# Grouped-query attention on one core: ten output staging buffers in place of four, and the copies of K into its padded form on the GpSimd DMA queue

## The chip, the cores and the metric

The kernel runs on one core of one Trainium2 chip. The metric is device time in microseconds (us) of one execution. The engines named below are PE (TensorE), ACT (ScalarE), DVE (VectorE), POOL (GpSimd) and SP (SyncE). SP does no arithmetic here: it only issues DMAs, in the order of its instruction stream, each when the semaphores it waits for have come.

## The reference

```python
batch, n_q_heads, n_kv_heads, seq, head_dim = (8, 8, 2, 1024, 64)
scale = 1.0 / np.sqrt(head_dim)
for g in range(n_kv_heads):                 # 4 query heads share one K and one V
    scores = scale * np.matmul(q_group, k_group.transpose(0, 1, 3, 2))
    scores_max = np.max(scores, axis=-1, keepdims=True)
    attn = np.exp(scores - scores_max)
    attn = attn / (np.sum(attn, axis=-1, keepdims=True) + 1e-08)
    output[:, q_start:q_end, :, :] = np.matmul(attn, v_group)
```

Inputs and output are float32; the kernel works in bf16 and takes no maximum off, since the scores are small.

## The kernel before, in words

A head's Q is 1024 x 64. It is cast to bf16 by a DMA from DRAM to DRAM on POOL's queue (`cast`, L248) and read back as 512 rows of 128 numbers, each row two neighbouring queries. Two transposing DMAs on SP (L260, 256 rows each) put it into SBUF as `qT`, 128 x 512: the upper 64 partitions hold the even queries, the lower 64 the odd ones. One job is one head and one `side` (even or odd queries), so there are 8 x 8 x 2 = 128 jobs of 512 queries.

K of a batch and group is cast and transposed in the same way into `kT`. A score matmul contracts over all 128 partitions and must see one side only, so K is kept with zeros in the other half of the partitions: `kset`, for each side. `place_k` (L267) copies `kT` there with four small DMAs (64 partitions x 512 bf16), one for each side and parity. There are 16 pairs of batch and group; the first is made on chip by `first_loads`, the other 15 come by `place_k`: 60 DMAs. V is read from its bf16 copy by two DMAs (`place_v`, L282). `kset` and `vset` have two sets, by the batch's parity.

A job has eight cells, one for each 128 keys. A cell's scores are one matmul (L351) into PSUM. 824 of the 1024 cells get their exponential on ACT (L362, two cells at a time, 412 instructions), 200 on DVE, where bits are put together (L371) and corrected for four cells at a time in four steps (L386, L392, L402, L406). Each cell's exponentials then go through four matmuls with V and a column of ones (L414), which gather output and row sums in one of two PSUM banks. When a job's eight cells are done, `normalise` takes the reciprocal of the sums (L427), multiplies into a staging tile `ost` (L429, 128 x 256 float32), and SP stores that tile (L435, 128 KB). The next multiply into the same staging buffer waits until that store has landed; a PSUM bank comes free for a later job when L429 has read it.

All is recorded in an order that `make_plan` writes out ahead of time. Casts, transposes, `place_k` and `place_v` are put in at fixed distances from the planned first use of a head, `th`:

```python
at(th - 28.0, cast, ("q", b, h), q[b, h])
at(th - 17.0 + n, transpose_q, b, h, n)
at(th - 38.0, cast, ("k", b, g), k[b, g])
at(th - 33.0, cast, ("v", b, g), v[b, g])
at(th - 27.0 + n, transpose_k, b, g, n)
at(th - 20.0, place_k, b, g, side, parity)
at(th - 15.0, place_v, b, g)
```

The order on each engine is the order of this plan. A cast also waits for the score matmul recorded last before it (`last_score`), so POOL's queue keeps pace with PE. SP has no such pace: it takes its DMAs one after another.

Of the kernel before, what the change touches and what calls it, by code (L numbers as in the profile page):

```python
# [162 lines left out]
def kernel(  # L163
# [7 lines left out]
    nc = tc.nc  # L171
# [38 lines left out]
    pa_pool = ctx.enter_context(tc.tile_pool(name="papool", bufs=26))  # L210
    pd_pool = ctx.enter_context(tc.tile_pool(name="pdpool", bufs=6))
    tmp_pool = ctx.enter_context(tc.tile_pool(name="tmppool", bufs=2))
    ostage_pool = ctx.enter_context(tc.tile_pool(name="ostage", bufs=4))
    recip_pool = ctx.enter_context(tc.tile_pool(name="recip", bufs=4))

    def psum_pools(name, n):
        return [
# [47 lines left out]
        transpose(("k", b, g), kT[(b, g)], n)  # L265

    def place_k(b, g, side, parity):  # L267
        nc.sync.dma_start(
            out=ksets[b % 2][
                side * D : (side + 1) * D, g, side, parity * HALF : (parity + 1) * HALF  # L270
            ],
            in_=kT[(b, g)][parity * D : (parity + 1) * D, :],
        )
# [179 lines left out]
    for b in range(B):  # L453
        for h in range(H):
            if b == 0 and h == 0:
                continue
            th = first_use[(b * H + h) * 2]
            if (b, h) != (0, 1):
                at(th - 28.0, cast, ("q", b, h), q[b, h])
            for n in range(HALF // PIECE):  # L460
                at(th - 17.0 + n, transpose_q, b, h, n)
            if h % HPG == 0:
                g = h // HPG
                at(th - 38.0, cast, ("k", b, g), k[b, g])
                at(th - 33.0, cast, ("v", b, g), v[b, g])
                for n in range(HALF // PIECE):
                    at(th - 27.0 + n, transpose_k, b, g, n)
                for side in range(2):
                    for parity in range(2):
                        at(th - 20.0, place_k, b, g, side, parity)  # L470
                at(th - 15.0, place_v, b, g)
# [34 lines left out]
```

## Time and profile before

| | |
|---|---|
| Time, median of 2 runs | 442.2 us (439.77 to 444.63) |
| The profiled execution: its time | 446.41 us |
| The profiled execution: its span | 444.6 us |
| Mean granted TensorE clock | 0.967 of full |

The span runs from the first to the last instruction; 1.8 us of the profiled execution's time lie around it. Idle time of an engine is put down to what ended it. A DMA issue counts as no engine's busy time, but the trace gives its start and how long the issuing queue was held by it, and when the data had landed.

### The profile page before, as it was taken

What the parts mean: (1) busy time and instruction counts of PE and PEld (TensorE: products, weight loads), DVE (VectorE), ACT (ScalarE), POOL (GpSimd) and SP (SyncE); (2) the same over time, 40 slices, a digit from 0 to 9 for tenths busy, and PEclk for the clock granted to TensorE, in tenths of its full rate; (3) what the DMA queues carried; (4) which work ended last, traced back from release to release, by engine and by line L of the source; (5) the groups of instructions that cost most, each with busy time, mean ns of one, the idle gap of its engine ahead of it and who ended that gap; (6) DMA issues with size and microseconds to landing.
All of it is one profiled execution on the core that took longest, in us unless ns stands there. A gap on an engine that the chain in (4) does not pass through costs nothing.

```text
span 444.6 us, 12769 instructions
## 1 busy us (share of the span) xinstructions
PE 383.3 (86%) x5132; PEld 235.5 (53%) x5132; DVE 376.2 (85%) x664; ACT 386.1 (87%) x415; POOL 55.8 (13%) x105
## 2 busy tenths in 40 slices
PE   4888799699998989898788969998969998797995
PEld 2445465355655546555455535565636665454654
DVE  5897698599997979699698859989959997897994
ACT  4898699599998979899899968998949999797992
POOL 5401001001111110111111110110101111100000
PEclk9999899799999989999999997999969999999998
DMA  3754666647665675656747555574655747645314
GB/s 94 125 98 94 115 110 111 116 91 126 100 125 104 111 119 97 120 93 114 119 84 126 109 107 102 97 130 97 121 107 98 119 83 135 111 89 111 82 29 84
DMA packets 137771, 46.73 MB, mean 105 GB/s; under 512 B 130848, under 2 KB 136224, under 8 KB 136224
## 3 DMA queue, kind: packets, MB, share of 16 engines
q1 hardware_dynamic: 134208, 33.46, 36.6%
q0 software_dynamic: 2976, 12.20, 20.9%
q8 instruction: 40, 0.66, 0.7%
q10 hardware_dynamic: 528, 0.26, 0.2%
q14 instruction: 19, 0.16, 0.1%
HBM read 27.13 MB, written 28.97 MB: 126 GB/s over the span
## 4 chain that ended last, share of the span: by engine, by line
DVE 32%; PE 26%; DMA 15%; ACT 13%; SPq 8%; issue 4%; POOL 1%; DVEq 0%; ACTq 0%
PE aps L351 14%; ACT pa L362 13%; DMA out_dram<-ost 11%; PE ops L414 9%; DVE y L402 7%; DVE pd L406 6%; SPq L260 6%; DVE pd L371 6%; DVE ost L429 5%; DVE y L392 4%; PE dps L351 3%; DVE z L386 2%; DMA qT<-scr_q 2%; DVE rec L427 1%; SPq L282 1%
## 5 line engine op out<-in xcount | busy, mean ns | idle before, releaser
L362 ACT ACTIVATE pa<-aps 128x1024 bf16<-128x1024 f32 x412 | 383.6, 1045 | 45.6 <-PE aps L351 44.0
L351 PE MATMUL aps<-qT,kset 128*128 128x512 bf16 x824 | 252.2, 389 | 13.5 <-ACT pa L362 9.7
L414 PEld LDWEIGHTS <-pa 128*128 128x128 bf16 x3296 | 137.7, 98 | 91.8 <-DVE ost L429 20.8
L414 PE MATMUL ops<-vset,pa 128*128 128x65 bf16 x3296 | 149.1, 195 | 29.5 <-DVE ost L429 29.4
L371 DVE TENSOR_SCALAR pd<-dps 128x512 uint16<-128x512 f32 x200 | 129.6, 680 | 2.4 <-PE dps L351 2.1
L351 PEld LDWEIGHTS <-kset 128*128 128x128 bf16 x1024 | 85.2, 99 | 68.1 <-issue 34.7
L429 DVE TENSOR_TENSOR ost<-ops,rec 128x256 f32<-128x256 f32 x128 | 54.3, 424 | 49.7 <-DMA out_dram<-ost 46.0
L248 POOL DMA_DIRECT2D scr_q<-in_q_dram x63 | 35.2, 558 | 300.7 <-PE aps L351 265.1
L351 PE MATMUL dps<-qT,kset 128*128 128x512 bf16 x200 | 66.6, 389 | 0.3
L406 DVE TENSOR_TENSOR pd<-pd,y 128x2048 uint16<-128x2048 uint16 x50 | 61.2, 1225 | 1.7
L402 DVE TENSOR_TENSOR y<-z,y 128x2048 f16<-128x2048 uint16 x50 | 61.2, 1225 | 1.7
L414 PEld LDWEIGHTS <-pd 128*128 128x128 bf16 x800 | 38.0, 97 | 39.4 <-DVE pd L406 20.1
L414 PE MATMUL ops<-vset,pd 128*128 128x65 bf16 x800 | 45.4, 194 | 8.5 <-DVE pd L406 7.4
L392 DVE TENSOR_SCALAR y<-z 128x2048 f16<-128x2048 uint16 x50 | 34.3, 687 | 0.6
L386 DVE TENSOR_SCALAR z<-pd 128x2048 uint16<-128x2048 uint16 x50 | 34.2, 684 | 0.0
L427 DVE RECIPROCAL rec<-ops 128x4 f32<-128x4 f32 x128 | 22.3, 174 | 5.5 <-PE ops L414 5.4
L248 POOL DMA_DIRECT2D scr_k<-in_k_dram x15 | 7.8, 519 | 22.7 <-PE aps L351 17.0
L248 POOL DMA_DIRECT2D scr_v<-in_v_dram x15 | 7.7, 515 | 15.8 <-PE aps L351 15.2
L321 PE MATMUL dps<-ident,hk 128*128 128x128 bf16 x8 | 1.0, 310 | 4.9 <-DVE hk L313 4.9
L309 POOL MEMSET kset<- 64x2048 bf16 x2 | 3.6, 1798 | 0.1
L321 PEld LDWEIGHTS <-hk 128*128 128x128 bf16 x8 | 0.8, 140 | 4.9 <-DVE hk L313 4.9
L236 DVE MEMSET kset<- 64x1024 uint32 x2 | 1.8, 912 | 1.3 <-PEq L490 1.0
(19 smaller groups left out, 7.9 us busy)
## 6 DMA issues: line engine op xcount, KB each, us to landing
out_dram<-ost SPq DMA_DIRECT2D x128, 128.0 KB, 2.7
scr_q<-in_q_dram POOLq DMA_DIRECT2D x63, 128.0 KB, 3.2
kset<-kT SPq DMA_DIRECT2D x60, 64.0 KB, 2.9
qT<-scr_q SPq DMA_TRANSPOSE x126, 3.5
scr_k<-in_k_dram POOLq DMA_DIRECT2D x15, 128.0 KB, 3.2
scr_v<-in_v_dram POOLq DMA_DIRECT2D x15, 128.0 KB, 3.7
vset<-scr_v SPq DMA_DIRECT2D x30, 64.0 KB, 3.2
kT<-scr_k SPq DMA_TRANSPOSE x30, 3.3
```

Source lines behind the costliest of these rows:

```text
L248: dma = nc.gpsimd.dma_start(out=scr.rearrange("(p f) -> p f", f=1024), in_=src.rearrange("(p s) d -> p (s d)", s=1024 // D),)
L260: nc.sync.dma_start_transpose(out=dst[:, rows], in_=src[rows, :])
L351: last_score[0] = nc.tensor.matmul(dst, lhsT=ksets[b % 2][:, h // HPG, side, c * 128 : (c + 1) * 128], rhs=qT[(b, h)], start=True, stop=Tr ...
L362: nc.scalar.activation(out=pt[:, 0:m], in_=psum.pop(("A", n))[:, 0:m], func=AF.Exp, scale=scale)
L371: nc.vector.tensor_scalar(out=groups[g][:, slot], in0=psum.pop(cell), scalar1=bits_scale, scalar2=bits_bias, op0=ALU.mult, op1=ALU.add,)
L386: nc.vector.tensor_scalar(out=z, in0=pd, scalar1=0x7F, scalar2=None, op0=ALU.bitwise_and)
L392: nc.vector.tensor_scalar(out=y, in0=temps[g][0], scalar1=CURVE_A / 128.0, scalar2=CURVE_B, op0=ALU.mult, op1=ALU.add,)
L402: nc.vector.tensor_tensor(out=y, in0=z, in1=y, op=ALU.mult)
L406: nc.vector.tensor_tensor(out=pd, in0=pd, in1=y, op=ALU.add)
L414: nc.tensor.matmul(ops_of[s][:, qs, :], lhsT=p_of[cell][:, qs * 128 : (qs + 1) * 128], rhs=vsets[b % 2][:, h // HPG, c, :], start=opens an ...
L427: nc.vector.reciprocal(out=rec, in_=o[:, :, D])
L429: nc.vector.tensor_tensor(out=ost, in0=o[:, :, 0:D], in1=rec.unsqueeze(2).to_broadcast([128, NQS, D]), op=ALU.mult,)
```

## The change

The pools of the staging tile `ost` and of the reciprocals get ten buffers in place of four. The four DMAs of `place_k` are issued by POOL in place of SP; their data, their shapes and what they wait for stay.

```diff
@@ -210,8 +210,8 @@
-    ostage_pool = ctx.enter_context(tc.tile_pool(name="ostage", bufs=4))
-    recip_pool = ctx.enter_context(tc.tile_pool(name="recip", bufs=4))
+    ostage_pool = ctx.enter_context(tc.tile_pool(name="ostage", bufs=10))
+    recip_pool = ctx.enter_context(tc.tile_pool(name="recip", bufs=10))
@@ -265,7 +265,7 @@
     def place_k(b, g, side, parity):
-        nc.sync.dma_start(
+        nc.gpsimd.dma_start(
             out=ksets[b % 2][
                 side * D : (side + 1) * D, g, side, parity * HALF : (parity + 1) * HALF
             ],
```

On SP, at the second of the 15 bursts of `place_k` (the DMAs into `kset_114`, the set of the odd batches), before (-) and now (+):

```order
 L260 DMA_TRANSPOSE kT<-scr_k 128x256 x2
 L260 DMA_TRANSPOSE qT<-scr_q 128x256 x2
-L435 DMA out_dram<-ost 128x4x64
-L268 DMA kset_114<-kT 64x512 x4
-L435 DMA out_dram<-ost 128x4x64 x2
+L435 DMA out_dram<-ost 128x4x64 x3
 L260 DMA_TRANSPOSE qT<-scr_q 128x256 x2
 L282 DMA vset_112<-scr_v 128x4x64 x2
```

The burst leaves SP, and the stores and transposes behind it follow one another.

On POOL, at the first burst (into `kset_109`, the set of the even batches; `scr_q`, `scr_k` and `scr_v` are the bf16 copies in DRAM that the casts write):

```order
 L248 DMA scr_q<-in_q_dram 16x4096
 L248 DMA scr_v<-in_v_dram 16x4096
-L248 DMA scr_q<-in_q_dram 16x4096 x3
+L248 DMA scr_q<-in_q_dram 16x4096 x2
+L268 DMA kset_109<-kT 64x512 x4
+L248 DMA scr_q<-in_q_dram 16x4096
 L248 DMA scr_k<-in_k_dram 16x4096
 L248 DMA scr_q<-in_q_dram 16x4096
 L248 DMA scr_v<-in_v_dram 16x4096
```

The burst now stands in POOL's order behind two casts and ahead of the third cast of Q and of the next cast of K; it waits there until `kT` has landed. All 15 bursts stand so.

On DVE, at the sixth and seventh stores into `ost`, with what each waits for:

```order
 L427 RECIPROCAL rec<-ops_524 128x4 [waits PE_49]
-L429 TENSOR_TENSOR ost<-ops_524,rec 128x256 [waits DMAHW4_49,DVE_49]
+L429 TENSOR_TENSOR ost<-ops_524,rec 128x256 [waits DVE_49]
 L371 TENSOR_SCALAR pd<-dps_614 128x512
 L386 TENSOR_SCALAR z<-pd 128x2048
 L427 RECIPROCAL rec<-ops_623 128x4 [waits PE_49]
-L429 TENSOR_TENSOR ost<-ops_623,rec 128x256 [waits DMAHW0_49,DVE_49]
+L429 TENSOR_TENSOR ost<-ops_623,rec 128x256 [waits DVE_49]
```

The waits for the landing of an earlier store (DMAHW) are gone here; from the eleventh job on they are there again, for the store ten jobs back. The order of PE, ACT and DVE is the same in both kernels.

## Rows read from the trace of the kernel before

**Rows 1.** The page: busy us of each engine, share, instructions.

```profile
PE 383.3 (86%) x5132; PEld 235.5 (53%) x5132; DVE 376.2 (85%) x664; ACT 386.1 (87%) x415; POOL 55.8 (13%) x105
```

**Rows 2.** Waits: who waited <- for whom: us, times, longest.

```profile
DVE ost L429 <- DMA out_dram<-ost: 46.0, 21, 5.1
ACT pa L362 <- PE aps L351: 44.0, 37, 4.5
...
PE ops L414 <- DVE pd L406: 7.4, 13, 0.9
...
PE aps L351 <- DMA qT<-scr_q: 1.7, 2, 1.3
```

**Rows 3.** Timeline, DVE, PE, ACT (start, us, line, count [idle before <-releaser]).

```profile
71.45 0.42 DVE L429 TENSOR_TENSOR ost<-ops,rec 128x256 f32<-128x256 f32 x1
...
85.30 0.42 DVE L429 TENSOR_TENSOR ost<-ops,rec 128x256 f32<-128x256 f32 x1 [4.73 <-DMA out_dram<-ost]
...
85.78 0.60 PE L414 MATMUL ops<-vset,pa 128*128 128x65 bf16 x8 [3.81 <-DVE ost L429]
...
87.33 1.02 ACT L362 ACTIVATE pa<-aps 128x1024 bf16<-128x1024 f32 x1 [4.48 <-PE aps L351]
```

**Rows 4.** Timeline of SP's queue between those two L429.

```profile
72.42 3.33 SPq L268 DMA_DIRECT2D kset<-kT  x4
75.85 0.54 SPq L435 DMA_DIRECT2D out_dram<-ost  x1
76.49 4.10 SPq L260 DMA_TRANSPOSE qT<-scr_q  x2
80.68 1.08 SPq L282 DMA_DIRECT2D vset<-scr_v  x2
81.85 1.01 SPq L435 DMA_DIRECT2D out_dram<-ost  x2
```

**Rows 5.** SP's queue: first and last row between 30 and 410, and the last transposes.

```profile
30.93 1.12 SPq L260 DMA_TRANSPOSE qT<-scr_q  x1
...
408.10 2.42 SPq L260 DMA_TRANSPOSE qT<-scr_q  x2
...
412.04 3.27 SPq L260 DMA_TRANSPOSE qT<-scr_q  x2
```

**Rows 6.** SP's queue: the first and the last burst of `place_k`.

```profile
22.42 3.85 SPq L268 DMA_DIRECT2D kset<-kT  x4
...
394.00 3.21 SPq L268 DMA_DIRECT2D kset<-kT  x4
```

**Rows 7.** Lines L260 and L248: ns of one issue, min/median/max.

```profile
L260 SPq DMA_TRANSPOSE qT<-scr_q x126: 1105/1228/3302, 6.1 to 414.1; - x126
...
L248 POOL DMA_DIRECT2D scr_q<-in_q_dram x63: 486/486/996, 1.3 to 398.9; - x63
```

**Rows 8.** Timeline: POOL's longest cast issue, and DVE beside it.

```profile
111.62 1.00 POOL L248 DMA_DIRECT2D scr_q<-in_q_dram  x1 [4.10 <-PE aps L351]
...
111.84 0.68 DVE L392 TENSOR_SCALAR y<-z 128x2048 f16<-128x2048 uint16 x1
```

**Rows 9.** POOL's casts behind the first and third burst; SP's issues that go with them.

```profile
16.79 0.49 POOL L248 DMA_DIRECT2D scr_k<-in_k_dram  x1 [1.74 <-PE aps L351]
...
69.65 0.49 POOL L248 DMA_DIRECT2D scr_q<-in_q_dram  x1 [5.25 <-PE dps L351]
...
15.71 3.13 SPq L260 DMA_TRANSPOSE kT<-scr_k  x2
...
39.30 2.44 SPq L260 DMA_TRANSPOSE kT<-scr_k  x2
...
87.39 1.13 SPq L260 DMA_TRANSPOSE qT<-scr_q  x1
```

**Rows 10.** DMA issues: KB each, median us from issue to landing.

```profile
scr_k<-in_k_dram POOLq DMA_DIRECT2D x15, 128.0 KB, 3.2
...
kT<-scr_k SPq DMA_TRANSPOSE x30, 3.3
```

## The prediction

> **What bounds the kernel now.** Busy time does not say: PE, DVE and ACT stand within 10 us of one another, each some 60 us under the span of 444.6 [rows 1]. The waits say more. DVE sat 46.0 us in 21 waits of L429 for a store to land, and ACT 44.0 us for scores [rows 2]. One stall read in order of time shows that these are one chain: the multiply at 85.30 waited 4.73 us, PE's output matmuls at 85.78 then had waited 3.81 us for it, and ACT at 87.33 had waited 4.48 us [rows 3].
>
> Why was the store late? The multiply at 85.30 needs the buffer of the job four before, filled at 71.45 [rows 3]. Its store was issued only at 81.85, ten microseconds after the data stood there. What SP did in between is [rows 4]: a burst of `place_k` (3.33 us), a store, two transposes (4.10), two loads of V (1.08), each starting some 0.1 us after the one before ended. SP never idled; the store stood in a line. And so through the run: the 202 rows of SP's timeline that start between 30 and 410, of which the first and the last are shown [rows 5], add up to 364.0 us in a stretch of 380, and the remaining 16 us are the tenth of a microsecond ahead of each. **SP's issue queue is full, and it is the bound.** DVE's wait for staging buffers is how the rest of the chip is held down to SP's pace. PE was held up for Q by only 1.7 us in two waits [rows 2], so SP was never so late that its transposes mattered much; the stores felt it first.
>
> **The change, part by part.**
>
> *Ten buffers.* L429 waits for a store ten jobs back in place of four. The 128 jobs share a span of 444.6 us, 3.5 us each, so a store may land some 30 us after its data stand before DVE feels it; the shown one took 13 us, from 71.87 to just before 85.30 [rows 3]. This takes the wait off DVE, but makes SP no shorter: by itself it would only hand the lateness to the transposes, for which PE would wait.
>
> *`place_k` off SP.* The 15 bursts hold SP 3.85 us (first) to 3.21 us (last) [rows 6]; all 15 rows add up to 50.1 us, and with 0.1 us ahead of each it is 51.6. That is time of the bounding queue, so it counts in full, unless the moved DMAs slow what stays.
>
> From these follow three ends for the span.
> - SP: its last transposes ended at 412.04 + 3.27 = 415.3 [rows 5], 29.3 us ahead of the end of the span. Without the bursts they can end at 415.3 - 51.6 = 363.7, so SP alone would allow 363.7 + 29.3 = 393.0.
> - DVE: 444.6 - 46.0 = 398.6 if all its waits for stores go [rows 2].
> - ACT: 444.6 - 44.0 = 400.6 if all its waits for scores go [rows 2].
>
> The largest stands: 400.6. All of ACT's gap cannot go, though. PE also waits 7.4 us for DVE's L406 [rows 2], which has nothing to do with stores, and with the other cover gone that reaches ACT. Between none and all of it I take half, 3.7 us: a span of 404.3, with 400.6 and 408.0 as this term's ends. For the granted clock, 0.967 of full over the span, I count nothing: what it costs lies within ACT's waits.
>
> *What POOL pays.* A cast holds POOL 0.49 us at the median, 1.00 at most [rows 7]. The trace has no `place_k` on POOL; I take 0.5 to 1.0 us each from those rows, 2 to 4 us a burst. POOL is busy 13% of the span [rows 1], so the 60 issues are hidden by its idle time. What is not plainly hidden is the wait. In POOL's new order a burst stands ahead of casts and waits for `kT` to land. At the first burst SP's `kT` transposes were issued from 15.71 to 18.84 and land 3.3 us after issue [rows 9, 10], so POOL stands until about 21 to 22 and is through with the burst at 24 to 26; the cast of K that ran at 16.79 [rows 9] moves 7 to 10 us later. Who waits for them? SP reads that K at 39.30; the cast lands 3.2 us after issue [rows 9, 10], so it may be some 19 us late. At the third burst the cast of Q at 69.65 is read at 87.39 [rows 9], 14 us after landing if that takes 3.2 us as K's does; SP issued the burst itself at 72.42 [rows 4], so on POOL it would be through by 74 to 76 at the latest, 5 to 7 us of delay. SP's lateness is the cover here. If SP catches up, the cover shrinks, but then `kT` lands earlier too and POOL waits less. I take zero; without cover a burst would cost up to 4 us, 60 in all.
>
> *A rule against this part.* POOL's longest cast issue, 1.00 us from 111.62, ended at 112.62, just behind DVE's L392 (111.84 to 112.52) [rows 8]. The Trainium skill, SBUF — State Buffer, Who interferes with whom, says that DVE and GpSimd take an exclusive lock on a shared port pair and the later one stands until the other is through; its advice is to issue DMAs from SP or ACT rather than from GpSimd. The trace agrees about the half microsecond. By the rule each moved DMA could cost up to one L392 of 0.68 us more, 41 us in all, but on POOL, which has it to spare; the sum stays.
>
> *The time.* 404.3 of span and 1.8 around it make 406.1 for an execution like the profiled one, which took 446.4 where the runs' median is 442.2. I take 3 of these 4.2 us off: **403 us**.
>
> **The rivals.**
>
> *SP gets back only half.* Transposes take 1.23 us at the median but up to 3.30 [rows 7]. The two at 76.49 took 4.10 [rows 4], 1.6 more than two medians, in a stretch with casts on POOL's queue. If each of the 15 bursts, now itself on POOL's queue, stretches SP's issues beside it by that much, SP loses 25 of the 51.6 us, and its end is 393.0 + 25 = 418. For it: the moved bytes still pass through the same DMA engines. Against it: they did so before. Its times are 410 to 428.
>
> *SP's issue time is not its own.* If SP is held by the DMA engines rather than by the number of its instructions, the freed 51.6 us are filled by longer issues of the others, and PE waits for Q in place of DVE for buffers: 442. Against it: the short stores in the same line (0.54 at 75.85 [rows 4]) show that most issues are not held. The Trainium skill, DMA: Bandwidth & Descriptors, Issuing engines are not separate DMA queues, says that issuing from several engines saves only sequencer time, usually small beside the DMA. That is this rival: the move would gain nothing, 442. The trace disagrees on "small": 364 us of issuing in 380.
>
> *POOL becomes the line that is waited in.* This one ends slower. A burst on POOL holds the casts behind it; SP then waits for a cast at its next transposes, with stores and the next `kT` behind them, and the next burst waits for that `kT`. It decides where a burst delays POOL by more than the 14 us that a cast waits to be read in mid-run, that is at about 3.5 us for each of the four DMAs, where casts show 0.49. At 5 us each, 20 a burst, 6 us are uncovered 15 times: 90 us on a span of 400.6, about 490. At 4.5 us each it is 60 us, about 460. Against it: the longest issue on POOL was 1.00 us.
>
> **How the numbers follow.** The forecast (three nearly equal bounds, 396 to 410) gets 0.66, half relief (410 to 428) 0.24, no relief 0.06, POOL as the line 0.04. The low end, 395, is DVE's 398.6 with 1.8 around it and the 4.2 us by which the profiled run lay above the median taken off, 396.2, less one for the spread of the runs. The high end goes into half relief as far as 422, since its first twelve microseconds hold most of its chance. Two per cent, about what a measurement of this kernel can tell from no change, is 433.4 to 451.0; forecast and half relief lie below, so 0.90 faster, 0.06 the same, 0.04 slower.
>
> **What would show it.** In the new profile L429 should wait for stores almost nowhere; SP's queue should show idle stretches, or still be full but with PE rarely waiting for `qT`; the bursts on POOL should take 2 to 4 us; ACT's busy share should pass 93%, and the clock's mean 0.98 of full. I am wrong if SP stays full and PE's waits for `qT` grow to tens of microseconds (rivals one and two), or if SP's transposes wait for casts (rival three).

## The result and the profile after

The changed kernel takes 397.55 us (median of 2 runs, 397.35 to 397.74) where the kernel before took 442.2: a ratio of 0.899, 95% interval 0.878 to 0.920. With more runs on one chip it was 397.5 against 444.54, ratio 0.894 (0.890 to 0.898). The profiled execution has a span of 395.6 us against 444.6, and a mean granted clock of 0.999 against 0.967.

The busy times, in the page's first part, answer [rows 1]:

```profile
span 395.6 us, 12683 instructions
...
PE 365.7 (92%) x5043; PEld 233.0 (59%) x5132; DVE 375.8 (95%) x664; ACT 381.5 (96%) x415; POOL 86.6 (22%) x165
```

PE, DVE and ACT do the same work in 49 us less. (89 of PE's 824 score matmuls have no record in this trace, x5043 for x5132, so its busy time reads somewhat low.) The waits (who waited <- for whom: us, times, longest) answer [rows 2]:

```profile
POOL kset L268 <- DMA kT<-scr_k: 68.7, 14, 8.6
...
PE aps L351 <- ACT pa L362: 13.6, 44, 0.6
...
ACT pa L362 <- PE aps L351: 1.3, 2, 1.1
...
PE aps L351 <- DMA qT<-scr_q: 0.3, 1, 0.3
```

DVE's 46.0 us for stores have no row any more, ACT's 44.0 us for scores have become 1.3, and PE now waits a little for ACT. The one long wait, POOL's for `kT`, is new. The stretch that held the shown stall [rows 3] now reads, in ACT's timeline and in the busy times of the stretch from 80 to 100 us (us, then PE, PEld, DVE, ACT and POOL busy with their counts, clock, DMA share, GB/s):

```profile
74.28 126.21 ACT L362 ACTIVATE pa<-aps 128x1024 bf16<-128x1024 f32 x137
...
80.00:100.00 20.00, 18.88 (x284) 12.40 (x288) 19.52 (x36) 20.00 (x23) 5.08 (x10) 1.00 0.78 127
```

137 exponentials run for 126 us without a gap. Before, the same stretch had PE 15.70, DVE 14.67 and ACT 14.61 us busy, at a granted clock of 0.83 of full: it fell from 2.4 to 1.2 GHz at 83.94, while PE stood in the wait of [rows 3], and came back at 90.77. In all, 31.6 us of the span before passed at 1.2 GHz, and of the changed kernel's only the last 2.5. SP's queue, beside [rows 4], has lost its bursts:

```profile
81.50 3.28 SPq L260 DMA_TRANSPOSE kT<-scr_k  x2
84.88 2.47 SPq L260 DMA_TRANSPOSE qT<-scr_q  x2
87.45 1.71 SPq L435 DMA_DIRECT2D out_dram<-ost  x3
89.27 3.53 SPq L260 DMA_TRANSPOSE qT<-scr_q  x2
92.90 1.55 SPq L282 DMA_DIRECT2D vset<-scr_v  x2
94.55 1.01 SPq L435 DMA_DIRECT2D out_dram<-ost  x2
```

It is still without a gap: its 174 rows that start between 30 and 360 us add up to 313.1 us, and with the tenth of a microsecond ahead of each they fill the stretch. A store is issued 4.8 us after its data stand (median over 128; before 6.55). But its last transposes now end at 367.3 in place of 415.3, and PE waits only 0.3 us for what they bring. On POOL, beside [rows 9], a burst takes 2.1 to 2.3 us (one of the 15 takes 5.6, since POOL stood idle 2.9 us within it), and the casts behind the first one came at 24.40 and 24.89 in place of 14.07 and 16.79:

```profile
22.12 2.29 POOL L268 DMA_DIRECT2D kset<-kT  x4 [8.64 <-DMA kT<-scr_k]
24.40 0.52 POOL L248 DMA_DIRECT2D scr_q<-in_q_dram  x1
24.89 0.53 POOL L248 DMA_DIRECT2D scr_k<-in_k_dram  x1
...
63.12 2.07 POOL L268 DMA_DIRECT2D kset<-kT  x4 [5.67 <-DMA kT<-scr_k]
65.18 0.52 POOL L248 DMA_DIRECT2D scr_q<-in_q_dram  x1
```

### The profile page after: what moved, and what is told of

It is laid out like the page before. It is cut to its first block, busy times and chain, and to the rows that moved or that the text cites. A ratio compares the mean times of both kernels' runs of the same rounds, so it can differ in the third digit from the quotient of the medians.

```text
span 395.6 us, 12683 instructions
## 1 busy us (share of the span) xinstructions
PE 365.7 (92%) x5043; PEld 233.0 (59%) x5132; DVE 375.8 (95%) x664; ACT 381.5 (96%) x415; POOL 86.6 (22%) x165
## 4 chain that ended last, share of the span: by engine, by line
ACT 67%; DVE 11%; PE 10%; issue 6%; DMA 3%; POOL 1%; SPq 0%
ACT pa L362 67%; PE ops L414 5%; PE aps L351 5%; DVE pd L371 3%; DVE y L402 2%; DVE pd L406 2%; DVE ost L429 1%; DMA vf<-in_v_dram 1%; PE dps L351 1%; DVE y L392 1%; DMA qT<-scr_q 1%; POOL kset L309 1%; DVE z L386 1%; DVE rec L427 1%; DMA scr_q<-in_q_dram 1%
## 5 line engine op out<-in xcount | busy, mean ns | idle before, releaser
L362 ACT ACTIVATE pa<-aps 128x1024 bf16<-128x1024 f32 x412 | 379.0, 1064 | 2.1 <-PE aps L351 1.3
L351 PE MATMUL aps<-qT,kset 128*128 128x512 bf16 x735 | 226.2, 379 | 15.5 <-ACT pa L362 13.6
L414 PEld LDWEIGHTS <-pa 128*128 128x128 bf16 x3296 | 134.5, 97 | 57.6 <-DVE ost L429 0.8
L414 PE MATMUL ops<-vset,pa 128*128 128x65 bf16 x3296 | 143.9, 193 | 3.4
L248 POOL DMA_DIRECT2D scr_q<-in_q_dram x63 | 34.0, 540 | 173.4 <-PE aps L351 150.6
L351 PE MATMUL dps<-qT,kset 128*128 128x512 bf16 x200 | 64.5, 380 | 1.0
L406 DVE TENSOR_TENSOR pd<-pd,y 128x2048 uint16<-128x2048 uint16 x50 | 61.2, 1225 | 1.7
L429 DVE TENSOR_TENSOR ost<-ops,rec 128x256 f32<-128x256 f32 x128 | 54.3, 425 | 4.4
L268 POOL DMA_DIRECT2D kset<-kT x60 | 32.2, 545 | 76.7 <-DMA kT<-scr_k 68.7
L392 DVE TENSOR_SCALAR y<-z 128x2048 f16<-128x2048 uint16 x50 | 34.3, 687 | 0.6
L386 DVE TENSOR_SCALAR z<-pd 128x2048 uint16<-128x2048 uint16 x50 | 34.2, 684 | 0.0
L248 POOL DMA_DIRECT2D scr_v<-in_v_dram x15 | 7.6, 505 | 8.2 <-PE aps L351 7.1
L248 POOL DMA_DIRECT2D scr_k<-in_k_dram x15 | 8.1, 542 | 4.7 <-PE aps L351 4.3
```

Source lines behind the costliest of these rows:

```text
L248: dma = nc.gpsimd.dma_start(out=scr.rearrange("(p f) -> p f", f=1024), in_=src.rearrange("(p s) d -> p (s d)", s=1024 // D),)
L268: nc.gpsimd.dma_start(out=ksets[b % 2][side * D : (side + 1) * D, g, side, parity * HALF : (parity + 1) * HALF], in_=kT[(b, g)][parity * D ...
L351: last_score[0] = nc.tensor.matmul(dst, lhsT=ksets[b % 2][:, h // HPG, side, c * 128 : (c + 1) * 128], rhs=qT[(b, h)], start=True, stop=Tr ...
L362: nc.scalar.activation(out=pt[:, 0:m], in_=psum.pop(("A", n))[:, 0:m], func=AF.Exp, scale=scale)
L386: nc.vector.tensor_scalar(out=z, in0=pd, scalar1=0x7F, scalar2=None, op0=ALU.bitwise_and)
L392: nc.vector.tensor_scalar(out=y, in0=temps[g][0], scalar1=CURVE_A / 128.0, scalar2=CURVE_B, op0=ALU.mult, op1=ALU.add,)
```

## The experiments

Each ran beside the kernel before on the same chip (444.1 to 445.1 us there).

| run | time, us | ratio to before (95%) | span | SP's DMA issues, sum |
|---|---|---|---|---|
| before (profile) | | | 444.6 | 381.3 |
| bufs_only | 437.0 | 0.983 (0.976 to 0.990) | 437.8 | 381.3 |
| half_place | 406.3 | 0.914 (0.908 to 0.920) | 402.4 | 344.5 |
| place_only | 401.4 | 0.904 (0.898 to 0.910) | 398.8 | 339.7 |
| changed kernel (after_again) | 397.5 | 0.894 (0.890 to 0.898) | 395.6 | 335.2 |
| place_six | 397.6 | 0.898 (0.890 to 0.905) | 396.0 | 337.5 |
| place_x4 | 398.4 | 0.900 (0.893 to 0.906) | 396.8 | 310.4 |
| v_too | 397.9 | 0.895 (0.890 to 0.900) | 396.0 | 301.0 |

The last column adds up how long each DMA issue held SP's queue. The span and the sum of the changed kernel are those of its first profile.

**Which half does it.** Ten buffers alone, then the move alone:

```diff
# bufs_only: the kernel before, with
+    ostage_pool = ctx.enter_context(tc.tile_pool(name="ostage", bufs=10))
+    recip_pool = ctx.enter_context(tc.tile_pool(name="recip", bufs=10))
```

> Ten buffers alone, place_k stays on SP. Theory 1 (SP's issue time is the bound of the kernel before, 364 us of issuing in 380): nothing leaves SP's queue, so the span stays at 436 to 446 us; DVE's 46.0 us of waits for stores shrink, and PE's waits for qT (1.7 us before) grow to some 40 us in their place. Theory 2 (four buffers were the bound, SP merely busy): DVE's waits go and nothing takes their place, 397 to 405 us.

```diff
# place_only: the changed kernel, with
+    ostage_pool = ctx.enter_context(tc.tile_pool(name="ostage", bufs=4))
+    recip_pool = ctx.enter_context(tc.tile_pool(name="recip", bufs=4))
```

> place_k on POOL alone, with four buffers. Theory 1 (SP's issue time): SP is relieved by 51.6 us, a store stands in line some 5 us as in the changed kernel, where four jobs at 3 us each leave 12 us for line and landing; a few waits for stores remain, under 10 us in all: 397 to 407 us. Theory 2 (the buffers): four buffers still hold DVE, 435 to 444 us.

Both came out as the theory of SP's issue time has it. The waits of bufs_only:

```profile
ACT pa L362 <- PE aps L351: 38.1, 30, 3.3
PE aps L351 <- DMA qT<-scr_q: 30.4, 18, 2.8
DVE rec L427 <- PE ops L414: 25.7, 29, 3.1
```

DVE no longer waits for stores, but PE's matmuls wait 30.4 us for Q, DVE for PE, and ACT nearly as long as before. SP's last transposes end at 414.9 (before 415.3): the wait has only changed its place. What the buffers did bring, 7 us of span, lies almost all behind that point, 22.9 us to the end in place of 29.3. The clock is no rival here: a run of bufs_only with a mean granted clock of 0.992 still took 436.6 us. In place_only DVE waits 4.4 us for stores in 6 waits, and the time is 4 us above that with ten buffers:

```profile
DVE ost L429 <- DMA out_dram<-ost: 4.4, 6, 1.5
```

**How much of SP's time counts.** Half of the burst goes back:

```diff
# half_place: the changed kernel, with
-        nc.gpsimd.dma_start(
+        (nc.sync if side == 0 else nc.gpsimd).dma_start(
```

> Ten buffers; two of each burst's four DMAs (side 0) go back to SP, two stay on POOL. Theory 1 (SP's issue time is paid in full): 30 DMAs at 0.86 us (51.6 us for 60) bring back 26 us. SP's last transposes in the changed kernel end near 366 us, then near 392, and with the 29.3 us behind them the span is 415 to 424 us; PE waits for qT some 20 us. Rival (SP has room left and only a whole burst hurts): 396 to 402 us.

406.3 us lies between the two. The 30 returned DMAs held SP 18.1 us (0.60 each, not 0.86), and the others shrank by nearly 9 us: the 30 transposes of K from 47.8 to 39.9 us, the stores from 84.1 to 81.2. So SP's last transposes end at 377.2, 10 us later than in the changed kernel and not 25. PE's matmuls wait 5.8 us for Q, in 4 waits. With ten buffers the first 30 DMAs cost 9 us and the other 30 cost 31 (bufs_only): the price of SP's time is not straight. Where SP is the bound it is nearly so: from half_place to bufs_only the sum of issues grows by 36.8 us and the span by 35.4.

**Six buffers.** 

```diff
# place_six: the changed kernel, with
+    ostage_pool = ctx.enter_context(tc.tile_pool(name="ostage", bufs=6))
+    recip_pool = ctx.enter_context(tc.tile_pool(name="recip", bufs=6))
```

> place_k on POOL with six staging buffers in place of ten. If a store needs the line on SP (median 4.8 us, at most 8.6 in the changed kernel) and 3.2 us to land, it is through within 12 us, and six jobs at 3 us give 18: no wait for a store, 396 to 399 us, the same as with ten. If ten buffers are needed because lateness comes in long stretches: waits of DVE for stores of over 5 us and 401 us or more.

397.6 us, and no row of DVE waiting for a store: with the burst gone from SP six are as good as ten.

**POOL's cover.** Each `place_k` in four parts:

```diff
# place_x4: the changed kernel, with
+        for p in range(0, D, 16):
+            nc.gpsimd.dma_start(
+                out=ksets[b % 2][
+                    side * D + p : side * D + p + 16, g, side, parity * HALF : (parity + 1) * HALF
+                ],
+                in_=kT[(b, g)][parity * D + p : parity * D + p + 16, :],
+            )
```

> The changed kernel with each place_k cut into four DMAs of 16 partitions: 240 issues on POOL in place of 60, same bytes. By the cover theory a burst takes POOL about 16 x 0.545 = 8.7 us in place of 2.2, casts behind it come up to 6.5 us later, and they are read 10 us (median) but at least 3.0 us after landing: a few stalls at most, 396 to 404 us. By the rival of the prediction (POOL becomes the line that is waited in) the cover is used up at every burst: over 410 us, with PE's waits for qT growing by more than 10 us.

398.4 us, under a microsecond more, with POOL 45% busy; PE waits 0.3 us for Q, in its weight loads. SP did wait: for 9 of the 63 heads it started the transposes of Q within 0.1 us of the landing of their cast, where the changed kernel has 2. So casts came too late for SP several times, and still not for PE.

**What bounds the changed kernel.** First SP, by moving V's loads too:

```diff
# v_too: the changed kernel, with
-            nc.sync.dma_start(
+            nc.gpsimd.dma_start(
                 out=vsets[b % 2][:, g, two * NHC : (two + 1) * NHC, 0:D],
```

> The changed kernel with the 30 loads of V on POOL's queue as well. Theory A (ACT, busy 381.5 of 395.6 us and idle 2.1 us ahead of its exponentials, is now the bound): SP is freed of another 20 us and its stores stand in line shorter than the 4.8 us median, with idle stretches on its queue, and the time stays at 396 to 399 us. Theory B (SP, whose rows fill 333 of 335 us between 30 and 365, is still the bound): 375 to 390 us.

397.9 us, no change, though SP's issues fall by 34 us in sum (V's loads had 19.0 of it; the stores fall by 16.7 as well) and its queue idles at last, as here for 3.1 us between two rows of its timeline:

```profile
229.12 1.17 SPq L260 DMA_TRANSPOSE qT<-scr_q  x1
233.43 0.37 SPq L435 DMA_DIRECT2D out_dram<-ost  x1
```

SP is not the bound of the changed kernel. Then, on the kernel of v_too, less work for ACT, for DVE, for both, and for PE as well:

```diff
# act_light: 52 cells' exponentials left out
-        m = len(cells)
+        m = 1 if n % 8 == 0 else len(cells)
...
-            p_of[cell] = pt[:, col, :]
+            p_of[cell] = pt[:, min(col, m - 1), :]
# dve_light: the step of L386 left out
-            z = tmp_pool.tile([128, GROUP, QBS], U16, name="z")[:, 0:m]
-            temps[g] = [z]
-            nc.vector.tensor_scalar(
-                out=z, in0=pd, scalar1=0x7F, scalar2=None, op0=ALU.bitwise_and
-            )
+            temps[g] = [pd]
...
-                scalar1=CURVE_A / 128.0,
+                scalar1=1e-4,
# three_light: act_light and dve_light, and the scores of those 52 cells
+            if col == 1 and n % 8 == 0:
+                return
```

> The kernel with V's loads on POOL too (397.85 us, SP out of the way), and every eighth ACT exponential takes one of its two cells; the other cell's output matmuls use the same exponentials. This leaves out 52 cells' exponentials, some 23 us of ACT. If ACT is the bound: 376 to 390 us, down to where DVE's 376 us of busy time stop it. If DVE holds it alone: 396 to 399 us.

> The same base, and DVE leaves out the 50 masking steps (L386, 0.68 us each, 34 us); the next step reads the unmasked bits. If ACT alone is the bound: 395 to 399 us, with DVE's busy share down from 95% to 87%. If DVE is a bound beside it, the time falls too: 380 to 394 us.

> The changed kernel as it is, beside these two on the same chip: 397 to 398 us.

> Both omissions together, 52 cells' exponentials on ACT and the 50 masking steps on DVE. Alone they gave 1.4 us and nothing, while ACT's busy time fell by 16.7 us and DVE's by 26. If ACT and DVE are two bounds side by side, each standing in when the other is lightened: 379 to 387 us, ACT's 364.8 us and the 14 us in which it idles at both ends. If a third bound (PE, at 92%) holds both: 393 to 398 us.

> As with both omissions, and the score matmul of the 52 cells whose exponentials are left out is left out too: 52 x 0.215 us, some 11 us of PE. The theory that ACT and DVE are the two bounds side by side has fallen (395.5 where 379 to 387 was expected). If PE, which shows matmuls back to back from 200 to 212 us there, is the third bound: 383 to 389 us. If it is neither of the three but the order in which they wait for one another: 392 to 396 us.

| run | time, us | busy PE / DVE / ACT, us |
|---|---|---|
| v_too | 397.9 | 365.4 / 376.2 / 381.5 |
| act_light | 396.1 | 363.5 / 375.0 / 364.8 |
| dve_light | 397.9 | 364.0 / 350.0 / 381.4 |
| both_light | 395.5 | 363.3 / 349.7 / 364.5 |
| three_light | 394.2 | 363.8 / 349.2 / 365.0 |

The changed kernel beside the first two took 397.5 us. These misses say most. Against v_too, ACT's work cut by 17 us gave 1.7; DVE's by 26 us nothing; both together 2.4; with some 11 us of PE's scores cut too, 3.6. (PE's busy time does not show that cut: the traces of the other four lack 89 records of score matmuls, that of three_light lacks none.) No engine's length is the bound by itself, and the theory of two bounds side by side fell. The chain of work that ended last, followed back from the last instruction, changes hands (shares of the span by engine): in the changed kernel it is

```profile
ACT 67%; DVE 11%; PE 10%; issue 6%; DMA 3%; POOL 1%; SPq 0%
```

in act_light

```profile
DVE 49%; PE 36%; ACT 8%; issue 4%; DMA 2%; ACTq 0%
```

and in three_light

```profile
ACT 59%; PE 33%; issue 6%; DMA 1%; DVE 0%; ACTq 0%
```

The waits of three_light show the other side:

```profile
PE aps L353 <- ACT pa L364: 15.1, 57, 0.6
ACT pa L364 <- PE aps L353: 14.7, 55, 0.7
```

PE waits for ACT 57 times and ACT for PE 55 times, a quarter of a microsecond each. With scores passing through two PSUM buffers in an order written ahead, each engine sets the pace in its own stretches. That it is this order is argued from these rows; no run changed the order or the number of PSUM buffers (all eight banks are taken), so it stays open.

## Why the prediction was right

**The bound.** That SP's issue queue holds the kernel before, and DVE's wait for buffers is only how it shows, is what bufs_only and place_only test, and both came out inside what this theory gave. Ten buffers alone moved DVE's wait to PE; the move without the buffers gave nine tenths of the gain. That SP's rows fill the run does not show it by itself: they fill it in the changed kernel too, where SP is not the bound. (The 364.0 us for 202 rows count three rows twice: it is 360.6 us for 199, with 18.9 us between them; the reading stands.) Whether an issue's time is SP's own work or a wait for the queue behind it, no run tells apart.

**The 51.6 us off SP.** The last transposes end 48.0 us earlier (415.3 to 367.3); predicted was 363.7. In v_too, where SP has room to spare, they end at 368.2: they now follow the plan's pace and not SP's load. That half_place paid only 10 us of a further 26 shows where the step "counts in full" is too simple: it holds only while SP is the bound, and a part of SP's issue time is stretch that gives way.

**ACT's end, 400.6, and the 3.7 us on it.** Here the sum was mis-sized, by 8.7 us of span. ACT's waits for scores fell from 44.0 to 1.3, so the term of the waits was right (42.7). The busy time, which the sum kept, fell too: 386.1 to 381.5 us, 4.6 less, since an exponential that follows another at once overlaps it (126.21 us for 137 is 0.92 each) and one that starts after a pause does not; 52 of the 412 did so before, 9 in the changed kernel. And half of the 7.4 us that PE's matmuls waited for L406 was to reach ACT: that wait has no row any more (PE's weight loads still wait 7.9 us for L406, 20.1 before), and none of it did. DVE's end of 398.6 fell likewise below: its other idle time shrank by 2.6 us with the stalls of PE. With that, 444.6 - 42.7 - 4.6 = 397.3; the remaining 1.7 us are idle time of ACT elsewhere.

**POOL.** `place_k` took 0.523 us at the median and 0.993 at most, inside the 0.5 to 1.0 taken. POOL waited 68.7 us for `kT`, as long as 8.64 us at the first burst, and the cast of K in [rows 9] came 8.1 us later, where 7 to 10 was given. Casts of Q are read about 10 us after landing (median; after the two at the start 1.5 at the least, behind the first burst, and then 3.0), so zero was right, and place_x4, which used this cover up several times, shows that more lies behind SP. The lock that the Trainium skill describes (SBUF — State Buffer, Who interferes with whom) shows in single issues: the longest, 0.993 us, ended 0.105 us after DVE's L386. It cost nothing here: DVE's L386 and L392 keep their means of 684 and 687 ns, and POOL has the time to spare.

**The rivals.** *SP gets back only half*: the DMAs that stayed on SP held it 333.3 us before (381.3 less the bursts' 48.0) and 335.2 after, so the moved bursts stretched them by 2 us, not 25. In the trace, the transposes of Q take 1.52 us (mean of 59) with only a cast in flight (from issue to landing), 1.23 (of 19) with only a burst and 1.37 (of 21) with neither; before it was 1.58 beside a cast and 1.24 without. Issues are longer beside casts, not beside bursts. *SP's issue time is not its own* falls with the same two sums and with place_only: the freed time was not filled. The sentence of the Trainium skill behind it (DMA: Bandwidth & Descriptors, Issuing engines are not separate DMA queues) holds in that only the sequencer's time is saved; that time was 42 us of the span (bufs_only against the changed kernel). Yet the rival had something: SP's queue stayed full after the change, and the same 316 DMAs held it 335 us there and 310 in place_x4. *POOL as the line that is waited in* needed 3.5 us for each DMA; there were 0.52, and four times as many did no harm.

**403 against 397.55.** The sum for an execution like the profiled one was 406.1, and the changed kernel's took 397.35: 8.7 us off, all in ACT's term. The 3 us taken off because the profiled run of before was slower than the median hid a part of it, and that was luck: the 442.2 was the median of two runs, and in the later comparisons, of seven runs each, the kernel before took 444.1 to 445.1. The changed kernel's two runs lie within 0.4 us of one another.

## What to carry to other kernels

An engine that waits for a buffer to be stored is not short of buffers if the store itself was issued late: look at what the issuing queue did between the data's end and the issue. A queue that only issues DMAs counts in no engine's busy time and can still be the bound: add up its rows, and see who waits for what it issues, since a full queue that nobody waits for is no bound. Moving a few DMAs to a queue that idled paid here up to the point where ACT, DVE and PE stood side by side; beyond it, less work for one of them or for all three gave 3.6 us at most.

## What the runs showed of the hardware that was not expected

The time for which an issue holds SP's queue is elastic. A transpose of 256 x 128 bf16 took 1.24 us in the mean with no cast in flight and 1.58 with one (before). In the changed kernel, place_x4 and v_too the same stores took 0.66, 0.53 and 0.53 us in the mean; the casts are the same in all three, so they are not the whole reason, which stays open. So a queue whose rows leave no gap need not be a bound: in the changed kernel the stretch from 30 to 360 us was filled, and 34 us less of issuing changed nothing.

ACT's exponentials of 128 x 1024 each take 1.06 us in the mean, but 0.92 us apiece when they follow one another. Every pause of ACT thus costs about a tenth of a microsecond beyond itself: 43 fewer pauses (52 before, 9 after) went with 4.6 us less busy time.
